# The joints of the first block: one wait for both norms' sums, three weights split ahead, two tiles grown together

## The chip, the cores and the metric

The kernel runs on one core of a Trainium2 chip. The metric is the device time of one execution in microseconds (us). Five engines work side by side, each through its own queue in order: PE (TensorE, matrix products), DVE (VectorE), ACT (ScalarE), POOL (GpSimd) and SP, which here only issues DMAs.

## The reference

Two stacks of layers run over 256 tokens of width 1024, in fp32. The first block has 16 extra "meta" tokens ahead (272 in all) and two layers, each a mixing layer and a feed-forward layer (FFN) with a convolution:

```python
for l in range(DEPTH):                       # DEPTH = 2
    u = _rms_norm(h, norm_mix_pre[l])
    (a_q, a_k, ..., gate_logits) = jnp.split(u @ w_in[l], offsets, axis=-1)
    ...                                      # four branches o_a, o_b, o_c, o_d
    merged = jnp.sum(jnp.einsum('btnw,nwd->btnd', branches, w_branch[l]) * gates, axis=2)
    h = h + _rms_norm(merged @ w_out[l], norm_mix_post[l])
    f = _conv_ffn(_rms_norm(h, norm_ffn_pre[l]), ffn_w_up[l], ffn_conv_w[l], ffn_conv_b[l], ffn_w_down[l])
    h = h + _rms_norm(f, norm_ffn_post[l])

def _rms_norm(x, g):
    y = x * lax.rsqrt(jnp.mean(x * x, axis=-1, keepdims=True) + NORM_EPS)
    return y * g
```

The second block (swiglu, convolution, pooling, and attention, under a condition vector) follows on the 256 tokens. What matters here is the pair of norms at every joint of the first block: norm 1 scales the result f of a layer's last product and adds it to h; norm 2 scales the new h for the first product of the next layer. There are four such joints: mixing to FFN and FFN to mixing in layer 0, mixing to FFN in layer 1, and FFN of layer 1 to the first swiglu of the second block.

## The kernel before, in words

Activations lie with the 1024 features on 128 partitions times 8 slices ("k") and the tokens along the free dimension. Every fp32 factor is split into a high and a low part: weights into wh and wl, inputs into uh and ul. A product is then three matmuls per slice: wh with uh, wh with ul, wl with uh. A 128x1024 weight tile (8 slices, 128 outputs) takes 24 matmuls.

Weights arrive by DMA as `raw` chunks of two tiles. ACT copies a tile into wh (`split`, L105), DVE takes the difference into wl (`split_low`, L118). `prefetch` (L129) does that ahead as long as a set of wh/wl is free: three sets (NS), plus "spare" ones in some stages. `get` (L154) hands over the next tiles. PSUM results are evicted by generators that `advance` (L178) moves on a step at a time. The written order of the code is the order of each engine's queue.

A joint goes as follows. `out_gemm` (L1524) makes the last product of a layer in 8 results j. `evict` writes f on ACT and, into a tile s, three sets of squares and products: f before the gain, squared; f squared; h times f. DVE adds those of j = 1 to 5 into the first. `post` then sums over the features with `summed` (L1577): matmuls with s as moving data and a column of ones as weights leave 32 equal rows, ACT copies them (L1590), and PE transposes them so that tokens lie on partitions (L1592). This is done first for norm 1, whose mean DVE scales (L269) and POOL raises to the power -1/2 (L271), then for the two sums of norm 2. `spread` (L274) turns the result r1 into a row for all partitions. For each slice k, DVE multiplies f (L1628), DVE or POOL adds it to h (L1630), ACT writes uh (`raw_hi`, L322) and DVE ul (`raw_lo`, L326).

`first_gemm` (L339) is the first product of the next layer. Its first group of tiles (`groups`: three tiles, or two in the second joint) runs on h times the gain, not yet scaled by norm 2 ("raw"), slice by slice as h comes. Meanwhile the power r2 is found. At the end of the group the inputs are written a second time, scaled (`normed`, L287, with `pr`, the spread r2), DVE scales the raw results (L385), and the remaining tiles run on the scaled inputs, one tile of 24 matmuls after another. `post` also ran `mid`, columns of the condition's modulation (`ada_some`, L1774, tiles adaw), which DVE makes in the out_gemm of the FFNs and in the swiglus.

## Time and profile before

| | us |
|---|---|
| median of 3 runs (2201.56 to 2204.61) | 2204.09 |
| profiled execution, own time | 2204.02 |
| its span, first to last instruction | 2202.0 |
| PE busy | 2137.4 (97%) |
| DVE busy | 1597.9 (73%) |
| mean granted clock of PE | 0.992 |

Times in the trace count from the start of the span. The four joints stand at 401 to 432, 615 to 653, 1005 to 1036 and 1207 to 1245 us. At full clock the matmuls of 272 columns begin 0.125 us apart, those of 256 columns 0.12 us; where the granted clock is 0.50, 0.226 us. A matmul's own 0.29 us overlap with those of its neighbours, so the pitch counts, not the sum of durations.

### The profile page before, as it was taken

How to read it: one execution, taken by the hardware profiler on the slowest of the kernel's cores; microseconds unless marked ns; L12 is line 12 of the kernel's file. 1: busy time of each engine (PE TensorE's matmuls, PEld its weight loads, DVE VectorE, ACT ScalarE, POOL GpSimd, SP SyncE). 2: the span in 40 equal slices, each digit the busy share in tenths (PEclk: the TensorE clock that was granted, in tenths of full speed). 3: DMA queues.
4: the chain of work that ended last, by engine and by line, in shares of the span. 5: the costliest groups of instructions: out<-in, count | busy, mean ns of one | idle time of the engine just before them, and what ended most of it. 6: DMA issues, size and time to landing. Idle time of an engine off the chain costs nothing. (4 is left out here: it accounts for less than half of the span.)

```text
span 2202.0 us, 42228 instructions
## 1 busy us (share of the span) xinstructions
PE 2137.4 (97%) x17234; PEld 2051.9 (93%) x17234; DVE 1597.9 (73%) x2833; ACT 1195.7 (54%) x2164; POOL 173.4 (8%) x223
## 2 busy tenths in 40 slices
PE   7999999999989999999999899999999999999998
PEld 7898989899979899898999899999999999989998
DVE  5665555888985656558989877797877877777553
ACT  4556454667456554547765644455544544476442
POOL 1320111100031101111000100001000000001000
PEclk9999999999999999999999999999999999999999
DMA  7653234454854342345559687555777687744552
GB/s 281 196 199 125 97 134 156 180 181 174 316 201 161 126 151 104 128 167 184 207 186 361 240 289 270 216 204 189 253 276 285 253 284 269 261 154 163 183 178 72
DMA packets 74322, 443.42 MB, mean 201 GB/s; under 512 B 14477, under 2 KB 15821, under 8 KB 26128
## 3 DMA queue, kind: packets, MB, share of 16 engines
q1 hardware_dynamic: 63312, 423.85, 53.7%
q0 software_dynamic: 10528, 16.79, 2.6%
q8 instruction: 135, 2.21, 0.4%
q14 instruction: 59, 0.48, 0.1%
q10 hardware_dynamic: 288, 0.07, 0.0%
HBM read 437.32 MB, written 10.01 MB: 203 GB/s over the span
## 5 line engine op out<-in xcount | busy, mean ns | idle before, releaser
L227 PE MATMUL g<-uh,wh 128*128 128x256 f32 (+2 forms) x3560 | 1028.0, 289 | 11.1 <-ACT uh L322 6.2
L227 PE MATMUL g<-ul,wh 128*128 128x256 f32 (+2 forms) x3560 | 1019.9, 286 | 10.8 <-DVE ul L326 6.3
L227 PE MATMUL g<-uh,wl 128*128 128x256 f32 (+2 forms) x3560 | 1016.6, 286 | 3.2 <-DVE wl L122 3.2
L122 DVE TENSOR_TENSOR wl<-raw,wh 128x1024 fp32r<-128x1024 f32 (+2 forms) x668 | 787.9, 1185 | 274.5 <-ACT wh L114 273.2
L114 ACT ACTIVATE wh<-raw 128x1024 fp32r<-128x1024 f32 (+2 forms) x668 | 678.3, 1020 | 348.3 <-PE g L227 313.7
L227 PEld LDWEIGHTS g<-uh,wh 128*128 128x128 f32 x3560 | 674.3, 189 | 34.1 <-issue 13.8
L227 PEld LDWEIGHTS g<-ul,wh 128*128 128x128 f32 x3560 | 673.1, 189 | 16.4 <-DVE ul L326 7.1
L227 PEld LDWEIGHTS g<-uh,wl 128*128 128x128 f32 x3560 | 675.1, 190 | 4.4 <-DVE wl L122 4.0
L227 PE MATMUL g<-gh,wh 128*128 128x256 f32 (+1 forms) x1056 | 299.2, 283 | 0.0
L227 PE MATMUL g<-gh,wl 128*128 128x256 f32 (+1 forms) x1056 | 299.2, 283 | 0.0
L227 PE MATMUL g<-gl,wh 128*128 128x256 f32 (+1 forms) x1056 | 299.0, 283 | 0.0
L227 PEld LDWEIGHTS g<-gl,wh 128*128 128x128 f32 x1056 | 201.5, 191 | 0.0
L227 PEld LDWEIGHTS g<-gh,wh 128*128 128x128 f32 x1056 | 201.3, 191 | 0.0
L227 PEld LDWEIGHTS g<-gh,wl 128*128 128x128 f32 x1056 | 201.3, 191 | 0.0
L1774 DVE CUSTOM_DVE_ANT_0 adaw<-adaw,condb,vec 128x1024 f32<-128x1024 f32 x144 | 182.4, 1279 | 0.0
L1677 DVE SCALAR_TENSOR_TENSOR y<-edge,vec,y 128x272 f32<-128x272 f32 (+1 forms) x176 | 86.4, 493 | 29.5 <-ACT y L1672 26.2
L227 PE MATMUL g<-oh,wh 128*128 128x272 f32 (+1 forms) x296 | 87.8, 297 | 0.0
L227 PE MATMUL g<-ol,wh 128*128 128x272 f32 (+1 forms) x296 | 84.8, 287 | 0.0
L227 PE MATMUL g<-oh,wl 128*128 128x272 f32 (+1 forms) x296 | 84.8, 286 | 0.0
L1920 ACT ACTIVATE sg<-g 128x256 f32<-128x256 f32 x80 | 30.5, 382 | 99.1 <-PE g L227 99.0
L1276 ACT ACTIVATE gt<-g 128x272 f32<-128x272 f32 (+1 forms) x64 | 25.1, 392 | 101.8 <-PE g L227 101.7
L1670 ACT ACTIVATE edge<-g 128x272 f32<-128x272 f32 (+1 forms) x82 | 32.3, 393 | 59.3 <-PE g L227 59.1
(384 smaller groups left out, 2311.5 us busy)
## 6 DMA issues: line engine op xcount, KB each, us to landing
raw<-in_weights_dram SPq DMA_DIRECT2D x298, 1024.0 KB, 5.0
adaw<-in_ada_t_dram SPq DMA_DIRECT2D x72, 1024.0 KB, 6.1
raw<-in_weights_dram SPq DMA_DIRECT2D x28, 768.0 KB, 5.0
skew<-scr POOLq DMA_DIRECT2D x6, 1086.0 KB, 23.0
h<-skew POOLq DMA_DIRECT2D x16, 272.0 KB, 3.7
h<-skew POOLq DMA_DIRECT2D x8, 512.0 KB, 5.2
condb<-cond SPq DMA_DIRECT2D x5, 512.0 KB, 4.7
hd<-h SPq DMA_DIRECT2D x2, 1088.0 KB, 8.9
```

Of the source, the lines that this page charges most:

```text
L114: self.nc.scalar.activation(h3[:, :, d0 : d0 + n], c.tile[:, :, c0 : c0 + n], AF.Copy)
L122: self.nc.vector.tensor_tensor(out=l3[:, :, d0 : d0 + n], in0=c.tile[:, :, c0 : c0 + n], in1=h3[:, :, d0 : d0 + n].bitcast(F32), op=SUB,)
L227: self.nc.tensor.matmul(out, lhsT, rhs, start=start, stop=stop, skip_group_check=True)
L1276: nc.scalar.activation(t[:, :rn], ps[:, :rn], AF.Tanh, scale=0.5)
L1670: nc.scalar.activation(e[:, 1 + r0 : 1 + r0 + rn], ps[:, :rn], AF.Copy)
L1677: nc.vector.scalar_tensor_tensor(out=y, in0=e[:, o : o + on], scalar=cw(i), in1=y, op0=MUL, op1=ADD)
L1774: self.nc.vector.tensor_tensor_reduce(out=t[:, i, :], in0=t[:, i, :], in1=self.condb, scale=1.0, scalar=self.v("ada_b_2", c), op0=MUL, op1 ...
L1920: nc.scalar.activation(t, ps[:, :SEQ], AF.Silu)
```

## The change

- **Sums.** DVE now adds the sets of all j (for norm 1 of j up to 5, the last two stay apart). Norm 1's sums are made with s as weights and the column of ones as moving data (`column`, 128x1), so they lie on partitions at once; the ACT copies and the transposes go. Norm 2's sums follow as six such columns, from the one accumulated tile, behind the spread.
- **Wait.** A copy `fence` on DVE stands behind the power. `warm` puts 2, 14 and 3 matmuls of 256 columns into a PSUM tile that nobody reads, between the sums and around the spread.
- **Weights.** The first three tiles of the next layer are split ahead into tiles of their own (`extra`, `places`): eh and el in the mixing stage, xwh/xwl and two of the adaw buffers in the FFN. The out_gemm's last piece splits up to four tiles; then `quiet` stops the prefetch until the raw group is over.
- **Raw group.** The slices from 4 on are scaled and added between the slices of the group (`steps`); per slice the group runs wh and wl with uh for its tiles, and wh with ul of the slice before. The power of norm 2 is asked for at k = 0, its spread stands at k = 5.
- **Groups.** The FFN's first gemm and the first swiglu's go from (3,) to (3, 2), the second mixing's from (2,) to (3, 2): after the raw group two tiles grow together, three matmuls of one and three of the other per slice.
- **Moved.** Pools are opened and closed, and the DMAs for it issued, after the raw group (`later`, `settle`). The modulation columns: 12 in place of 24 in each FFN, and 40, 32, 40, 8 in place of 32, 32, 32, 0 and the rest in the swiglus; 144 in all as before.

```diff
+            extra = self.extra.get(self.n_split)
+            spare = extra is None and c.spare > 0 and c.spare == self.phase and sum(out) < self.n_spare
+            if extra is None and not spare and len(out) - sum(out) >= NS:
                 break
             while c.tile is None and self.lows:
                 self.split_low()
             if c.tile is None:
                 break
-            self.split(self.n_split, spare)
-            self.where[self.n_split] = spare
+            self.split(self.n_split, spare, extra)
+            if extra is None:
+                self.where[self.n_split] = spare
...
-        self.prefetch(max(2, first + n - self.n_split + 1))
+        need = first + n - self.n_split
+        if need > 0 or not self.quiet:
+            self.prefetch(max(need, 0 if self.quiet else 2, 0 if self.quiet else need + 1))
...
+    def warm(self, ps, n):
+
+        if self.n_used in self.split_tiles:
+            w = self.split_tiles[self.n_used][0]
+            for _ in range(n):
+                self.mm(ps[: w.shape[2], :SEQ], w[:, 0, :], self.ul[:, KD - 1, META:T])
...
+            late = raw and g == 0 and len(self.steps) > 0
+            after = after or late
+            pss = [(self.gps if i < (2 if after else 3) else self.aps)() for i in range(size)]
...
+            def low(k):
+                for (w, m0, m1), ps in zip(tiles, pss):
+                    self.mm(ps[: m1 - m0, : n + c0], w[0][:, k, m0:m1], self.ul[:, k, t], False, k == KD - 1)
+
             for k in range(KD):
+                t = slice(c.start - c0, c.stop)
                 for (w, m0, m1), ps in zip(tiles, pss):
-                    self.mm3(
-                        ps[: m1 - m0, : n + c0], w, k, m0, m1, (self.uh, self.ul), k, c.start - c0, n + c0,
-                        k == 0, k == KD - 1,
-                    )
-                if raw and g == 0 and k == 1:
+                    o, xh, xl = ps[: m1 - m0, : n + c0], self.uh[:, k, t], self.ul[:, k, t]
+                    self.mm(o, w[0][:, k, m0:m1], xh, k == 0, False)
+                    if late:
+                        self.mm(o, w[1][:, k, m0:m1], xh, False, False)
+                        continue
+                    self.mm(o, w[0][:, k, m0:m1], xl, False, False)
+                    self.mm(o, w[1][:, k, m0:m1], xh, False, k == KD - 1)
+                if late:
+                    if k:
+                        low(k - 1)
+                    if self.steps:
+                        self.steps.popleft()()
+                    if k == 0:
+                        r, bl = sums()
+                    if k == KD - 1:
+                        low(k)
+                        self.settle()
+                        self.quiet = False
+                elif raw and g == 0 and k == 1:
                     r, bl = sums()
-                elif raw and g == 0 and k == 2:
+                if raw and g == 0 and k == (5 if late else 2):
...
+            raw_now, raw = raw, raw and g < len(groups) - 1 and not late
+            if not raw_now:
...
-            self.prefetch(2)
+            if late:
+                c0 = 0
+            self.prefetch(1 if late else 2)
...
-            cols(3552, 768, evs, groups=(2,) if first == "D" else ())
+            cols(3552, 768, evs, groups=(3, 2) if first == "D" else ())
...
+            if j == 0:
+                S["acc"] = s
+            elif j >= KD - 2:
+                S["late"] = S.get("late", []) + [s]
+            if j == KD - 1:
+                yield
...
+            if j:
+                acc, q = S["acc"], 0 if j < KD - 2 else 1
+                nc.vector.tensor_tensor(out=acc[:, q:3, c], in0=acc[:, q:3, c], in1=s[:, q:3, c], op=ADD)
...
+        def places(i):
+
+            if kt == KD:
+                return [self.q4(nm, F32R).rearrange("p a b -> p (a b)")[:, :1024] for nm in ("eh", "el")]
+            if i == 0:
+                return [self.ff.tile([128, 1024], F32R, tag=nm, name=nm, bufs=1) for nm in ("xwh", "xwl")]
+            t = self.ff.tile([128, 2, D], F32R, tag="adaw", name="ew", bufs=2)
+            return t[:, 0, :], t[:, 1, :]
...
+                    self.extra = {self.n_used + 2 * n_pieces + i: lambda i=i: places(i) for i in range(3)}
...
+                    if n == n_pieces - 1:
+                        self.prefetch(4 - 4 * i)
+                        self.quiet = True
                     (wt,) = self.get()
...
-            r1 = self.pow_rsqrt(summed([0], self.w1(), pt)[:, 0], nb, D, "r1")[:, :nb]
-            self.prefetch(1, ahead=3)
-            self.drain()
-            pt = self.aps()
-            sums = summed([1, 2], self.w1(), pt)
...
+            pw, ps = self.gps(), self.aps()
+            self.mm(ps[:, 0:4], self.ident, self.zero4, True, False)
+            for i, s in enumerate([S["acc"]] + S["late"]):
+                for b, (t0, n) in enumerate(bl):
+                    column(ps[:, b : b + 1], s[:, 0, :], t0, n, False, i == 2)
+                self.warm(pw, (0, 2, 14)[i])
+
+            g = self.pipes.popleft()
+            next(g)
+            next(g)
+            r1 = self.pow_rsqrt(ps[:, :nb], nb, D, "r1")[:, :nb]
+            fence = self.sm.tile([128, 4], F32, tag="fence", name="fence", bufs=2)
+            nc.vector.tensor_copy(fence[:, :nb], r1)
+            for _ in g:
+                pass
             p1 = self.spread(r1, bl)
+            ps2 = self.aps()
+            for q in range(2):
+                for b, (t0, n) in enumerate(bl):
+                    column(ps2[:, 4 * q + b : 4 * q + b + 1], S["acc"][:, 1 + q, :], t0, n, True, True)
+            self.warm(pw, 3)
...
+            def step(k):
+                def fn():
+                    if k < KD:
+                        value(k, nc.gpsimd)
+                    self.raw_lo(k - 2)
+
+                return fn
+
+            self.before_norm(gain(), shift and shift(), c, second, [step(k) for k in range(4, KD + 2)])
             if shift:
                 self.raw_shift(self.mod[:, 0:8])
-            for k in range(KD):
-                nc.vector.tensor_tensor(out=f[:, k, c], in0=f[:, k, c], in1=p1[:, c], op=MUL)
-                eng = nc.gpsimd if k else nc.vector
-                eng.tensor_tensor(out=self.h[:, k, c], in0=self.h[:, k, c], in1=f[:, k, c], op=ADD)
-                self.raw_hi(k)
-                if k == 2:
-                    R["r2"] = second()
-                if k > 1:
-                    self.raw_lo(k - 2)
-            self.raw_lo(KD - 2)
-            self.raw_lo(KD - 1)
+            value(0, nc.vector)
+            value(1, nc.gpsimd)
+            self.raw_lo(0)
+            value(2, nc.gpsimd)
+            value(3, nc.gpsimd)
+            self.raw_lo(1)
...
-                self.add(self.gemm(x, one * 3, ev, r0, rn, groups=(3,)), *[ch for _, ch in begun], cg)
+                self.add(self.gemm(x, one * 3, ev, r0, rn, groups=(3, 2)), *[ch for _, ch in begun], cg)
...
-            lambda: self.ada_some(2),
+            lambda n: self.ada_some(2 if n < 2 else 1 if n < 10 else 0),
...
-            c = {(0, 0): 48, (0, 2): 80, (1, 0): 112}.get((i, s))
-            self.ada_begin(range(c, c + 32) if c else ())
+            self.ada_begin(range(*{(0, 0): (24, 64), (0, 2): (64, 96), (1, 0): (96, 136), (1, 2): (136, 144)}[i, s]))
...
+                self.add(self.gemm(x, m * 3, ev3, META, SEQ, groups=(3, 2)), *[ch for _, ch in begun], cg)
```

PE, from the last product of mixing 0 (g, the last wl) to the first raw matmul, before (a are PSUM tiles, s4 the squares, ones32 the ones, r1 the power):

```order
L227 MATMUL g_4587<-uh_81,wl_4551 128x272
L1584 MATMUL a_4660<-s4_4405,ones32_90 32x272
L1584 MATMUL a_4660<-s4_4619,ones32_90 32x272
L1584 MATMUL a_4660<-s4_4655,ones32_90 32x272
L1592 MATMUL a_4658<-ident_89,w1_4659 128x32 x3
L1584 MATMUL a_4680<-s4_4405,ones32_90 32x272 x2
L1584 MATMUL a_4680<-s4_4619,ones32_90 32x272 x2
L1584 MATMUL a_4680<-s4_4655,ones32_90 32x272 x2
L1592 MATMUL a_4678<-ident_89,w1_4679 128x64 x3
L227 MATMUL a_4691<-ident_89,r1_4670 128x16
L227 MATMUL a_4691<-ident_89,r1_4670 128x128 x2
L227 MATMUL g_4760<-uh_81,wh_4588 128x272
L227 MATMUL g_4760<-ul_82,wh_4588 128x272
```

After (eh, el are the tiles split ahead; the rows into g_4670 are the `warm` ones):

```order
L245 MATMUL g_4593<-uh_81,wl_4553 128x272
L245 MATMUL a_4671<-zero4_94,ident_89 128x4
L245 MATMUL a_4671<-ones32_90,s4_4407 128x1 x3
L245 MATMUL a_4671<-ones32_90,s4_4637 128x1 x3
L245 MATMUL g_4670<-ul_82,eh_4555 128x256 x2
L245 MATMUL a_4671<-ones32_90,s4_4667 128x1 x3
L245 MATMUL g_4670<-ul_82,eh_4555 128x256 x14
L245 MATMUL a_4708<-ident_89,r1_4703 128x16
L245 MATMUL a_4708<-ident_89,r1_4703 128x128 x2
L245 MATMUL a_4712<-ones32_90,s4_4407 128x1 x6
L245 MATMUL g_4670<-ul_82,eh_4555 128x256 x3
L245 MATMUL g_4736<-uh_81,eh_4555 128x272
L245 MATMUL g_4736<-uh_81,el_4556 128x272
```

Three 32-row sums, three transposes, six more sums and three more transposes stood ahead of the spread; now nine columns and sixteen `warm` matmuls do, and six columns behind it.

PE, the end of the raw group and what follows in the FFN of layer 0, before:

```order
L227 MATMUL g_4762<-uh_81,wh_4672 128x272
L227 MATMUL g_4762<-ul_82,wh_4672 128x272
L227 MATMUL g_4762<-uh_81,wl_4673 128x272
L227 MATMUL g_4904<-uh_81,wh_4757 128x272
L227 MATMUL g_4904<-ul_82,wh_4757 128x272
L227 MATMUL g_4904<-uh_81,wl_4758 128x272
L227 MATMUL g_4904<-uh_81,wh_4757 128x272
L227 MATMUL g_4904<-ul_82,wh_4757 128x272
L227 MATMUL g_4904<-uh_81,wl_4758 128x272
```

After:

```order
L245 MATMUL g_4737<-ul_82,eh_4594 128x272
L245 MATMUL a_4738<-ul_82,eh_4597 128x272
L245 MATMUL g_4922<-uh_81,wh_4600 128x272
L245 MATMUL g_4922<-ul_82,wh_4600 128x272
L245 MATMUL g_4922<-uh_81,wl_4601 128x272
L245 MATMUL g_4923<-uh_81,wh_4903 128x272
L245 MATMUL g_4923<-ul_82,wh_4903 128x272
L245 MATMUL g_4923<-uh_81,wl_4904 128x272
L245 MATMUL g_4922<-uh_81,wh_4600 128x272
L245 MATMUL g_4922<-ul_82,wh_4600 128x272
```

Before, 24 matmuls of the fourth tile follow each other; now the fourth tile's first three are followed by three of the fifth (wh_4903, wl_4904).

ACT at the same place, after (the last of the eight scaled inputs, the fifth tile's wh, the results' evictions, the sixth's wh):

```order
L322 ACTIVATE uh_81<-w1_4884 128x272
L322 ACTIVATE uh_81<-w1_4888 128x272
L322 ACTIVATE uh_81<-w1_4892 128x272
L127 ACTIVATE wh_4903<-raw_4586 128x1024
L1754 ACTIVATE edge0_4856<-w1_4897 128x272
L1756 ACTIVATE y_4908<-w1_4897,vec_100 128x272
L1754 ACTIVATE edge1_4857<-w1_4899 128x272
L1756 ACTIVATE y_4911<-w1_4899,vec_100 128x272
L1754 ACTIVATE edge2_4858<-w1_4901 128x272
L1756 ACTIVATE y_4914<-w1_4901,vec_100 128x272
L127 ACTIVATE wh_4916<-raw_4586 128x1024
```

Before, at that place on ACT:

```order
L304 ACTIVATE uh_81<-w1_4863 128x272
L304 ACTIVATE uh_81<-w1_4867 128x272
L304 ACTIVATE uh_81<-w1_4871 128x272
L114 ACTIVATE wh_4882<-raw_4581 128x1024
L114 ACTIVATE wh_4885<-raw_4581 128x1024
L1670 ACTIVATE edge0_4748<-w1_4876 128x272
L1672 ACTIVATE y_4893<-w1_4876,vec_98 128x272
```

The fifth tile's wh stands behind the eight scaled inputs in both orders; before, it was the first of two.

## Rows read from the trace of the kernel before

**Rows 1.** The page's busy times over the whole span.
```profile
PE 2137.4 (97%) x17234; PEld 2051.9 (93%) x17234; DVE 1597.9 (73%) x2833; ACT 1195.7 (54%) x2164; POOL 173.4 (8%) x223
```

**Rows 2.** PE's waits: line waited at, releaser, us in total, times, longest.
```profile
PE g L227 <- DVE ul L326: 6.3, 4, 1.6
PE g L227 <- ACT uh L322: 6.2, 4, 1.6
PE a L1592 <- ACT w L1590: 3.9, 8, 0.5
PE g L227 <- DVE wl L122: 3.2, 3, 1.2
PE a L701 <- ACT dv L993: 1.6, 1, 1.6
```

**Rows 3.** The first transition's timeline: start, duration, engine, line, operation, [idle before].
```profile
401.19 0.29 PE L227 MATMUL g<-uh,wl 128*128 128x272 f32 x1
...
404.10 1.00 POOL L271 TENSOR_TENSOR r<-ms,mhalf 128x3 f32<-128x3 f32 x1 [26.94 <-DVE ms L269]
...
406.21 1.03 PE L227 MATMUL a<-ident,r 16*128 16x16 f32 x6
407.28 0.44 DVE L1628 TENSOR_TENSOR f<-f,a 128x272 f32<-128x272 f32 x1 [1.68 <-PE a L227]
...
408.80 0.40 PE L227 MATMUL g<-uh,wh 128*128 128x272 f32 x1 [1.56 <-ACT uh L322]
```

**Rows 4.** Windows, first and third transition: length, busy by engine, granted clock, DMA.
```profile
410.64:414.05 3.41, 3.27 (x14) 3.27 (x15) 3.41 (x9) 1.06 (x3) 3.41 (x5) 0.50 0.00 0
414.06:422.20 8.14, 8.14 (x65) 7.97 (x64) 7.07 (x21) 4.67 (x10) 1.83 (x2) 1.00 0.65 205
...
427.50:431.90 4.40, 4.40 (x23) 4.40 (x24) 4.29 (x8) 4.38 (x10) 0.00 (x0) 0.61 0.47 147
...
1029.40:1033.50 4.10, 2.96 (x24) 2.75 (x24) 4.03 (x7) 4.10 (x9) 0.00 (x0) 1.00 0.44 138
```

**Rows 5.** Timeline, first transition, from the last normed input to the fifth tile.
```profile
424.36 0.43 ACT L304 ACTIVATE uh<-w 128x272 fp32r<-128x272 f32 x1 [0.33 <-DVE w L302]
...
424.70 1.99 ACT L114 ACTIVATE wh<-raw 128x1024 fp32r<-128x1024 f32 x2
...
425.18 1.13 DVE L385 TENSOR_TENSOR w<-g,pr 128x272 f32<-128x272 f32 x3
...
426.23 2.35 DVE L122 TENSOR_TENSOR wl<-raw,wh 128x1024 fp32r<-128x1024 f32 x2
...
427.50 0.43 PE L227 MATMUL g<-uh,wl 128*128 128x272 f32 x1 [1.19 <-DVE wl L122]
```

**Rows 6.** Timeline, second transition: a modulation column, first raw matmul, two waits.
```profile
617.86 1.28 DVE L1774 CUSTOM_DVE_ANT_0 adaw<-adaw,condb,vec 128x1024 f32<-128x1024 f32 x1
...
623.67 0.39 PE L227 MATMUL g<-uh,wh 128*128 128x272 f32 x1 [1.56 <-ACT uh L322]
...
640.39 0.39 PE L227 MATMUL g<-uh,wl 128*128 128x272 f32 x1 [0.84 <-DVE wl L122]
...
652.98 0.44 PE L701 MATMUL a<-ident,dv 128*128 128x128 f32 x2 [1.59 <-ACT dv L993]
```

**Rows 7.** Timeline and windows, fourth transition.
```profile
1211.51 0.14 DVE L269 TENSOR_SCALAR ms<-a 128x2 f32<-128x2 f32 x1
...
1223.86 4.63 DVE L122 TENSOR_TENSOR wl<-raw,wh 128x1024 fp32r<-128x1024 f32 x4 [0.46 <-ACT wh L114]
...
1216.19:1223.00 6.81, 5.44 (x25) 5.44 (x26) 6.16 (x16) 3.67 (x8) 5.85 (x8) 0.50 0.40 168
1229.00:1236.00 7.00, 5.36 (x26) 3.39 (x24) 6.50 (x18) 3.94 (x8) 0.00 (x0) 1.00 0.39 162
1239.00:1245.00 6.00, 5.80 (x50) 5.60 (x48) 4.86 (x7) 5.41 (x9) 0.00 (x0) 1.00 0.60 195
```

**Rows 8.** The same windows' columns, most of the next stage.
```profile
1250.00:1500.00 250.00, 247.73 (x2070) 246.21 (x2068) 208.27 (x337) 125.20 (x189) 3.82 (x3) 1.00 0.68 242
```

More of the change, by code (lines that the diff above doesn't have):

```diff
@@ L79, in add, with later, settle @@
         self.items.append((fn, chunks))
+    def later(self, fn):
+        self.items.append((lambda: self.deferred.append(fn), ()))
+    def settle(self):
+        while self.deferred:
+            self.deferred.pop(0)()
     def start_stream(self):
@@ L103, in pump_dma, with split @@
             self.n_dma += 1
-    def split(self, j, spare):
+    def split(self, j, spare, extra=None):
         c, s = self.subq[j]
@@ L138, in prefetch @@
             out = [x for k, x in self.where.items() if self.held or k >= self.n_used]
-            spare = c.spare > 0 and c.spare == self.phase and sum(out) < self.n_spare
-            if not spare and len(out) - sum(out) >= NS:
+            extra = self.extra.get(self.n_split)
+            spare = extra is None and c.spare > 0 and c.spare == self.phase and sum(out) < self.n_spare
+            if extra is None and not spare and len(out) - sum(out) >= NS:
                 break
@@ L367, in first_gemm @@
                     nc.scalar.activation(pr, ps[:, o : o + n], AF.Copy)
-                elif k in (4, 6):
+                elif not late and k in (4, 6):
                     self.prefetch(1)
@@ L371, in first_gemm @@
                 yield
-            self.held = False
-            if not raw:
+            self.held, self.norm = False, None
+            raw_now, raw = raw, raw and g < len(groups) - 1 and not late
+            if not raw_now:
                 for i, ps in enumerate(pss):
@@ L379, in first_gemm @@
                 continue
-            if g == len(groups) - 1:
+            if not raw:
                 self.normed(self.h[:, :, c], pr, gain, shift, n, (self.uh[:, :, c], self.ul[:, :, c]))
@@ L411, in setup @@
         nc.vector.memset(self.zero, 0.0)
+        self.zero4 = c.tile([128, 4], F32, name="zero4")
+        nc.vector.memset(self.zero4, 0.0)
         self.mhalf = c.tile([128, 16], F32, name="mhalf")
@@ L756, in pool_open @@
             S["merged"] = self.mx.tile([128, KD, T], F32, tag="merged", name="merged", bufs=1)
-        self.add(pool_open)
+        (self.later if l else self.add)(pool_open)
         if l == 0:
@@ L779, in pre @@
             nc.sync.dma_start(out=self.hd[l], in_=self.h)
-        self.add(pre)
+        (self.later if l else self.add)(pre)
         def to(name, i, w=128):
@@ L1512, in mixing @@
         )
-        self.add(lambda: self.mx_guard.__exit__(None, None, None))
+        self.later(lambda: self.mx_guard.__exit__(None, None, None))
     def down_chunks(self, w, kt):
@@ L1661, in pool_open @@
                 nc.vector.memset(t[:, T + 1 : T + 2], 0.0)
-        self.add(pool_open)
+        self.later(pool_open)
         def conv(j, ps):
@@ L1718, in conv_ffn @@
         self.add(self.ada_end)
-        self.add(lambda: self.ff_guard.__exit__(None, None, None))
+        self.later(lambda: self.ff_guard.__exit__(None, None, None))
     def out_gemm_ff(self, w, S, o0, on, l):
@@ L1877, in gated_gemm @@
             return
-        for ch, j0, k0, nk, first, last in self.down_chunks(w, kt):
+        for n, (ch, j0, k0, nk, first, last) in enumerate(self.down_chunks(w, kt)):
             def fn(j0=j0, k0=k0, nk=nk, first=first, last=last):
@@ L1898, in gated_gemm @@
             self.add(fn, ch)
-            if kt == KF:
-                self.ada_some()
+            if kt == KF and n < 10:
+                self.ada_some(2)
     def swiglu(self, i, s, f, nxt):
@@ L1934, in swiglu, with ev3 @@
             cu = self.wcols(self.w["ffn_w_up_2"][i, f], j * 128, 256)
+            if j == 0 and i + s == 0:
+                begun = [(evg, cg), (evu, cu)]
+                continue
+            if j == 2 and i + s == 0:
+                def ev3(q, ps, evs=[e for e, _ in begun] + [evg]):
+                    return evs[q // 2](q % 2, ps)
+                self.add(self.gemm(x, m * 3, ev3, META, SEQ, groups=(3, 2)), *[ch for _, ch in begun], cg)
+                self.add(self.gemm(x, m, evu, META, SEQ), cu)
+                self.ada_some(2)
+                continue
             if j == 0:
@@ L1937, in both @@
                     return (evg if q < 2 else evu)(q % 2, ps)
-                self.add(self.gemm(x, m + m, both, META, SEQ, groups=(4,) if i + s else (3,)), cg, cu)
+                self.add(self.gemm(x, m + m, both, META, SEQ, groups=(4,)), cg, cu)
                 continue
@@ L2359, in opened @@
             self.xp, self.n_spare, self.phase = self.xp_guard.__enter__(), 5, phase
-        self.add(opened)
+        self.later(opened)
         for i in range(2):
```

74 lines of the change are left out of this document (33 added, 41 removed).

## The prediction

> **What bounds the kernel now.** The page's busy times come first: PE works 97% of the span [rows 1]. Nearly all the time is matmuls that the change leaves alone, so only stretches where PE waits or runs at half clock can give anything. The list of PE's waits says where these are [rows 2]: at the four joints PE waits 1.6 us each for the first uh and 1.6 us each for the first ul, the ACT copies ahead of the transposes add 3.9 us over eight waits, and the weights' low parts 3.2 us over three. That is 19.6 us over all joints, under 1% of the time; beside it stands the half clock. Then the timelines of the joints show which engine each wait hangs on [rows 3, 5, 6, 7], and the windows what PE does there and at what clock [rows 4, 7].
>
> In the first joint the last product starts at 401.19, the power at 404.10, the spread at 406.21 and the first raw matmul at 408.80 [rows 3]. Then PE stands until 410.78 for ul and runs at half clock (0.50, which is 1.2 of 2.4 GHz) for 3.4 us, 14 matmuls [rows 4]. The raw group's 72 matmuls are issued by 422.2. The scaled inputs are written meanwhile, the last uh at 424.36; only behind it does ACT split the fifth tile and the sixth, and DVE their low parts, so PE waits until 427.50 with 98 of 120 matmuls done (72 raw, 24 of tile four, 2 of tile five) [rows 5]. The rest runs at a mean clock of 0.61 [rows 4] and the 120th matmul is through at 431.9. I use the 120th matmul as the mark for each joint, since after it PE goes on without waits in the FFNs.
>
> **The change part by part.** The sum is made against the profiled execution's own time, 2204.02 us (span 2202.0), which stands 0.07 us below the median of 2204.09; nothing has to be moved between the two.
>
> *Sums and wait, joints one and three.* The ACT copies, the transposes and the 32-row sums go. What comes instead: a zeroing and nine columns. No row shows a column behind these squares; between the pitch of a matmul (0.12) and the 0.26 of a 32-row sum (six in 1.56) the ten cost 1.2 to 2.6 us; I take 2.2. They can't start at once: DVE has splits in its queue and only then the adds of the accumulated squares, by about 402.2 (a low part costs 1.2 us [rows 5], and one more of them stands there than before). So columns end near 404.5, mean 0.16, power 1.00 [rows 3], that is 405.7. But the 14 warm matmuls stand on PE ahead of the spread: 404.5 + 14 x 0.12 = 406.2, the same as before. The first raw matmul comes at 408.8 again, between 0.5 us earlier and 0.5 later. The fence costs DVE nothing by itself, since DVE has only the spread to wait for; at most the two last adds, 0.9 us, are late, and they feed norm 2, which is needed much later.
>
> *Raw group.* Six matmuls per slice need uh alone, so the wait for ul goes, and with PE fed the clock should stay full. The bound is then POOL's chain of h, 0.9 us per slice with a power of 1.0 between, and the late spread at slice 5. By this chain the raw group ends at 420.4 in place of 422.2.
>
> *Two tiles together.* Here the order of the queues decides [the rows of order above]. After the raw group PE has three matmuls of the fourth tile and then meets the fifth, whose wh stands on ACT behind the eight scaled inputs as before. These are paced by DVE and start when `pr` is there, 418.4 against 418.6. So wh is ready about 425.6 (424.7 + 1.0 of the two in 1.99), wl behind the three scaled results about 427.3 (426.23 + half of 2.35, less 0.1) [rows 5]. Before, PE used the time from 422.2 to 425.8 for the whole fourth tile; now it stands. At 427.3 it has done 72 + 3 + 2 = 77 of 120, and 43 remain: 43 x 0.125 = 5.4 us at full clock, 432.7, which is 0.8 us later than before. If the clock falls as in 427.50 to 431.90 (0.61 over 4.4 us [rows 4]), 4.4 x 0.39 = 1.7 us more. Joint one: +0.8 to +2.5, and I take +2.
>
> *Joint three* is the same with one difference: before, it kept full clock over its wait of 1.2 us (3.2 less 1.19 and 0.84 [rows 2, 5, 6]) and after it (1.00 over 1029.40 to 1033.50 [rows 4]) and was through at 1033.5. With wl at 1030.8 the change is through at 1030.8 + 5.4 = 1036.2, or 1.7 later. +2.7 to +4.4; I take +3.2.
>
> *Joint two.* The mean waited behind two modulation columns of 1.28 us [rows 6]; these go, and the spread is then bound by the warm matmuls, 1 us earlier than before. Five tiles are ready here (three ahead and two in ordinary sets, since the FFN's own spare set holds one of the last product's), so the two tiles together don't stand: first raw matmul 622.6 (623.67 [rows 6] less 1), raw group 11.6 us as in joint one (408.8 to 420.4), to 634.3, 48 more matmuls to 640.3, the 120th. Before, it came at 646.2 after a split's wait until 640.39 [rows 6]. Of these 5.9 us most is given back: the sixth and seventh tiles are split behind the scaled inputs, and the chain ACT-DVE-ACT of the keys to dv, which ended at 652.98 [rows 6], moves only as far as its own work lets it, to about 650. That is 3 us, less 1.7 if PE's rest brings the half clock. -1.3 to -3; I take -2.2.
>
> *Joint four.* Two columns go from before the mean (1211.51), so f starts 2.3 us earlier; the stretch of 6.8 us at clock 0.50 [rows 7], 25 matmuls, would run at full; and four low parts in a row, 4.63 us, no longer delay the scaled inputs. The raw group, some 10.6 us with 258 columns, ends at 1224.0 in place of 1229, the two ready tiles to 1229.8. Then PE waits for the sixth tile, whose low part follows the three scaled results: about 1233.1. 48 x 0.12 = 5.8 gives 1238.9, or 1240.4 with some half clock, for the 168th, which before came at 1244.6 and a wait of 0.4 later (last window of [rows 7]). -4.6 to -6.2; I take -5.
>
> *Moved work.* 24 modulation columns move from the FFNs to the second block, 24 x 1.28 = 31 us of DVE. There PE is busy 247.7 of 250 us and DVE 208.3 [rows 8]; 8 more columns in that stage are 10 us, which leaves DVE at 88%. Cost nothing; without the cover up to 1.28 us for each late tile. DMAs that move behind the raw group (condition, modulation, the edge of h) pass only each other on SP and POOL; the weight chunks, three ahead, are freed earlier. The group of tiles in the swiglu and its tables cost the same matmuls.
>
> Sum: +2 + 3.2 - 2.2 - 5 = -2.0, so 2202.0. The ends: +0.8 + 2.7 - 3 - 6.2 = -5.7 and, with another 0.5 us at each first matmul, +2.5 + 4.4 - 1.3 - 4.6 + 1 = +2.0: 2198.3 to 2206.0.
>
> **The rivals.** *A: the joints keep what they gain.* The gain at the 120th matmul stays in joints two and four (-5.9; 1239 to 1229.8 = -9.2), and one and three lose only 0.8 and 2.7: -11.6, 2192.4. For it speaks that PE is the bound after every joint [rows 1, 8]; against it the chain to dv in joint two and the sixth tile's split, which stand behind the same scaled inputs. 17%.
>
> *B: slower, by the clock.* The longer rests, some 6 us in joints one and three and 3 us in two and four, could each be followed by as long a stretch at 0.50 as joint four has, 6.8 us [rows 7], and not by 3.4. That costs 3.4 us per joint: +4.2, +6.1, +0.4, -2.8, together +7.9, 2211.9. It decides once PE stays at half clock for a second stretch of that length. For it: the longest rests of PE in any joint stand here. Against it: joint three's wait of 1.2 us brought no half clock at all [rows 4]. 15%.
>
> The Trainium skill ("TensorE: Matmul & The Clock Gate", Part 1) says that a PE left idle falls to 1.2 GHz and, kept busy, comes back to 2.4 GHz; by that rule each of the new rests ends at half clock, as rival B has it, and the warm matmuls help only ahead of the raw group. The trace agrees in joints one, two and four and not at joint three's second wait.
>
> *C: the change doesn't do what it says.* POOL's h paces the raw group whatever PE does, now with a second power early in its queue; PE rests in each slice and the raw group ends as before. Then joint one and three stay at +2 and +3.2 (they hang on the fifth tile, not on the raw group), joint two gives -1 and joint four -3: +1.2, 2205.2. For it: POOL is busy all of 410.64 to 414.05 (3.41 of 3.41 [rows 4]). Against it: that stretch's PE is at half clock and short of ul too. 16%.
>
> **How the numbers follow.** 52% for the forecast, 17, 15 and 16 for A, B and C. A measurement of this kernel can tell 0.2%, 4.4 us, from no change; that is 2199.6 and 2208.5. Faster: all of A and a quarter of the forecast's cases (those with joint four near -6 and joint one near +1), 0.17 + 0.13 = 0.30. Slower: two thirds of B and a little of C, 0.10 + 0.03 = 0.13. The rest, 0.57, is the same. For 8 in 10 the range covers the forecast's own 2198.3 to 2206.0 and C, half of A and most of B: 2194 to 2210.
>
> **What would show it.** Right: in the FFNs' first gemm PE stands about 6 us after three matmuls of the fourth tile, waiting for ACT's wh and DVE's wl; the waits for ul after the first raw matmul are gone; the clock is 1.00 in the raw groups; the first swiglu's 168th matmul comes about 5 us earlier against the last product before it. Wrong: if the fifth tile is ready when the raw group ends (then joints one and three gain, too), if the second block shows PE waiting for modulation or splits, or if the half clock follows the rests for 6.8 us.

## The result, and the profile after

The changed kernel takes 2225.11 us (median of 4 runs, 2221.83 to 2225.97) against 2204.35 us before: a ratio of 1.0096, 95% interval 1.0081 to 1.0111. It is slower by some 21 us, outside the range forecast. The profiled execution of after is the quickest of the four, 2221.83 us with a span of 2219.8; against the 2202.0 of before that is 17.8 us.

By the page's busy times PE has 8.7 us more [rows 1], about what the 76 warm matmuls ask for at 0.12 us each (9.1, an estimate); so 9 of the 17.8 us are PE standing still.

```profile
PE 2146.1 (97%) x17334; PEld 2071.8 (93%) x17334; DVE 1603.7 (72%) x2851; ACT 1194.3 (54%) x2156; POOL 173.9 (8%) x223
```

PE's waits, as in [rows 2] (line waited at, releaser, us in total, times, longest):

```profile
PE g L245 <- ACT wh L127: 11.2, 3, 4.7
PE a L245 <- ACT s L1600: 8.8, 2, 4.5
...
PE a L757 <- ACT dv L1049: 3.9, 1, 3.9
PE g L245 <- DVE wl L135: 3.8, 5, 0.9
...
PE g L245 <- DVE sg L2008: 2.4, 1, 2.4
PE g L245 <- ACT uh L348: 2.3, 10, 0.4
```

What the change was to remove is removed: the raw groups' waits for ul and those for the ACT copies no longer stand there, and that for uh falls from 6.2 to 2.3 us. But 11.2 us for a weight's wh are new, and 8.8 us for s, the squares of the last results, and 2.4 us for sg, which DVE makes from the first swiglu's results; only then are their PSUM tiles free. The largest two are worth a look at their places.

Joint two, ACT's timeline (start, duration, operation, [idle before]):

```profile
617.70 1.06 ACT L127 ACTIVATE xwh<-raw 128x1024 fp32r<-128x1024 f32 x1 [9.65 <-PE g L245]
618.66 1.99 ACT L127 ACTIVATE ew<-raw 128x1024 fp32r<-128x1024 f32 x2
620.56 1.99 ACT L127 ACTIVATE wh<-raw 128x1024 fp32r<-128x1024 f32 x2
622.45 0.38 ACT L1600 ACTIVATE s<-g 128x272 f32<-128x272 f32 x1
```

And PE's, at the same place:

```profile
622.88 1.44 PE L245 MATMUL a<-ones,s 128*128 128x1 f32 x6 [4.30 <-ACT s L1600]
...
625.89 3.33 PE L245 MATMUL g<-ul,xwh 128*128 128x256 f32 x14
629.15 1.39 PE L245 MATMUL a<-ident,r 16*128 16x16 f32 x6
```

Before, ACT had its splits done and wrote the last squares 0.3 us after the last product (615.70):

```profile
616.02 0.40 ACT L1542 ACTIVATE s<-g 128x272 f32<-128x272 f32 x1 [0.22 <-PE g L227]
```

In the changed kernel ACT stands 9.65 us before it may write xwh, until the last product (617.50) is through: xwh is the FFN's spare set, and the last tile of the out_gemm lies in it. Behind this one instruction stand four more splits, 5 us in all, and behind these the squares of the last results, which the columns want. Then the fourteen warm matmuls run at half clock, 3.33 us in place of 1.9, and the spread behind them starts 2 us after the power is done (626.30 + 0.86). Joint four shows the same (xwh from 1220.55, a wait of 4.5 us).

Joint one goes the way the prediction told, within 0.2 us, until the fifth tile is there: 26.2 us after the last product, forecast 26.1. PE's wait behind the raw group, and the clock around it, in views that answer to [rows 5] and [rows 4]:

```profile
424.45 0.59 PE L245 MATMUL g<-uh,wh 128*128 128x272 f32 x1 [4.69 <-ACT wh L127]
...
426.15 0.60 PE L245 MATMUL g<-uh,wl 128*128 128x272 f32 x1 [0.88 <-DVE wl L135]
```

```profile
407.75:419.20 11.45, 10.87 (x80) 10.03 (x79) 10.21 (x30) 4.95 (x11) 6.68 (x8) 1.00 0.22 49
419.20:426.15 6.95, 1.38 (x7) 0.83 (x5) 6.72 (x17) 5.26 (x12) 0.00 (x0) 0.69 0.72 297
426.15:434.30 8.15, 8.15 (x44) 8.15 (x45) 5.31 (x9) 4.67 (x7) 0.00 (x0) 0.64 0.37 131
1015.73:1019.14 3.41, 3.41 (x16) 3.21 (x16) 0.94 (x3) 0.00 (x0) 0.86 (x1) 0.50 0.33 135
```

The raw group runs at full clock, as forecast. Then PE does 7 matmuls in 6.95 us, and the 44 that follow take 8.15 us at a mean clock of 0.64; before, a mean of 0.61 lasted for 4.40 us [rows 4]. In joint three the clock falls already ahead of the raw group (fourth line), is back for it, and falls again in the wait for the fifth tile.

To compare versions I count, in each joint, from the start of the last product's last matmul to the moment when the next gemm's first 264 matmuls (raw group included) are done, read as the start of the 265th. "At the 120th" and "at the 168th" are read in the same way. By then each kernel has done the same work. These times are read from each version's trace:

| us to the 264th matmul | joint 1 | joint 2 | joint 3 | joint 4 | sum |
|---|---|---|---|---|---|
| before | 48.9 | 55.1 | 45.5 | 49.4 | 198.8 |
| after | 52.4 | 62.1 | 51.4 | 53.7 | 219.6 |
| e1 own buffer | 52.6 | 54.1 | 54.6 | 47.0 | 208.3 |
| e2 one by one | 51.2 | 62.0 | 50.3 | 49.6 | 213.0 |
| e3 fifth first | 47.2 | 63.6 | 50.8 | 56.4 | 218.1 |
| e4 = e1 + e3 | 47.2 | 56.4 | 50.8 | 49.9 | 204.3 |
| e5 = e4, no warm | 47.8 | 56.7 | 47.9 | 50.4 | 202.8 |
| e6 = e4, swiglu as before | 48.7 | 56.7 | 49.2 | 44.6 | 199.2 |
| e7 before, in twos | 52.5 | 55.1 | 49.8 | 50.1 | 207.4 |
| e8 = e6, no warm | 47.8 | 57.2 | 47.6 | 44.3 | 196.9 |
| e9 = e8, raw group of 2 | 47.8 | 53.4 | 47.7 | 44.6 | 193.3 |
| e10 before, columns moved | 47.3 | 55.0 | 45.5 | 47.8 | 195.5 |
| e11 joint 4 alone | 47.2 | 54.6 | 47.1 | 44.2 | 193.0 |

The sum after is 20.8 us over that of before; 3 us come back between the joints, where the trace of before has two stretches of 3.4 us at half clock (from 820.24 and 1970.54) that the trace of after has not. One joint's time in one trace is good to 1.5 us at best: joint one has the same instruction order in before and e10 and reads 48.9 and 47.3, and joint three has it in after and e1 and reads 51.4 and 54.6, with half clock at other places.

Each version was timed beside the kernel before, whose median was 2204.35 us beside the changed kernel, 2201.39 beside e1 to e4, 2202.54 beside e5 to e8 and 2202.01 beside e9 to e12. Versions of different groups are therefore compared by what each has over its own before; the changed kernel has 20.8 us.

### The profile page after: what moved, and what is told of

Read it like the earlier page. It is cut to its first block, busy times and chain, and to the rows that moved or that the text cites. A ratio compares the mean times of both kernels' runs of the same rounds, so it can differ in the third digit from the quotient of the medians.

```text
span 2219.8 us, 42473 instructions
## 1 busy us (share of the span) xinstructions
PE 2146.1 (97%) x17334; PEld 2071.8 (93%) x17334; DVE 1603.7 (72%) x2851; ACT 1194.3 (54%) x2156; POOL 173.9 (8%) x223
## 5 line engine op out<-in xcount | busy, mean ns | idle before, releaser
L245 PE MATMUL g<-uh,wh 128*128 128x256 f32 (+2 forms) x3464 | 1000.8, 289 | 18.0 <-ACT wh L127 11.2
L245 PE MATMUL g<-ul,wh 128*128 128x256 f32 (+2 forms) x3464 | 988.9, 285 | 2.8 <-DVE ul L1560 2.8
L245 PE MATMUL g<-uh,wl 128*128 128x256 f32 (+2 forms) x3464 | 985.8, 285 | 3.8 <-DVE wl L135 3.8
L135 DVE TENSOR_TENSOR wl<-raw,wh 128x1024 fp32r<-128x1024 f32 (+4 forms) x656 | 772.1, 1182 | 261.9 <-ACT wh L127 261.2
L127 ACT ACTIVATE wh<-raw 128x1024 fp32r<-128x1024 f32 (+4 forms) x656 | 665.6, 1019 | 343.6 <-PE g L245 298.4
L245 PEld LDWEIGHTS g<-uh,wh 128*128 128x128 f32 x3464 | 653.6, 189 | 39.9 <-issue 16.0
L245 PEld LDWEIGHTS g<-uh,wl 128*128 128x128 f32 x3464 | 656.0, 189 | 5.4 <-DVE wl L135 5.0
L245 PEld LDWEIGHTS g<-ul,wh 128*128 128x128 f32 x3464 | 654.5, 189 | 4.1 <-DVE ul L1560 3.7
L2003 ACT ACTIVATE sg<-g 128x256 f32<-128x256 f32 x80 | 30.6, 382 | 100.0 <-PE g L245 100.0
```

The costliest lines, as they stand in the source:

```text
L127: self.nc.scalar.activation(h3[:, :, d0 : d0 + n], c.tile[:, :, c0 : c0 + n], AF.Copy)
L135: self.nc.vector.tensor_tensor(out=l3[:, :, d0 : d0 + n], in0=c.tile[:, :, c0 : c0 + n], in1=h3[:, :, d0 : d0 + n].bitcast(F32), op=SUB,)
L245: self.nc.tensor.matmul(out, lhsT, rhs, start=start, stop=stop, skip_group_check=True)
L2003: nc.scalar.activation(t, ps[:, :SEQ], AF.Silu)
```

## The experiments

**e1.** Joints two and four: another buffer for the first weight split ahead (and `y` 6, `gg` 4 buffers, for room).

```diff
-                return [... for nm in ("xwh", "xwl")]
+                return [... for nm in ("zwh", "zwl")]
```

> One edit at joints two and four: the first of the three weights split ahead gets a buffer of its own in place of the spare set's, which the last product's last tile still holds (y from 8 to 6 buffers and gg from 6 to 4 make room for it). Theory 1: in the changed kernel ACT waits for the end of the last product before it may write that first weight (617.70 in joint two), and four more splits and then the last results' squares stand behind it; with a buffer of its own the splits run before the product ends, and the first column after the wait comes about 5 us earlier in joints two and four: spread about 6 us after the last product in place of 11.65 and 10.55, total about -9 us, near 2216. Rival 1: it is the five splits as such (5.1 us of ACT) that hold the squares, whenever they may start, because the raw chunks come late: then under 2 us change, 2223 or more. Rival 2: what costs is the half clock after PE's rests; then the spread comes earlier but the 264th matmul does not, and the time moves by less than 3 us.

Measured: 2211.60 us (6 runs), 1.0045 [1.0031, 1.0060] of before. That is 10.2 us over its before, 10.6 less than the changed kernel has. The spread comes 4.33 us after the last product in joint two (11.65) and 4.63 in joint four (10.55). ACT's timeline of this run shows why:

```profile
608.23 1.04 ACT L127 ACTIVATE zwh<-raw 128x1024 fp32r<-128x1024 f32 x1
...
614.77 1.06 ACT L127 ACTIVATE wh<-raw 128x1024 fp32r<-128x1024 f32 x1 [1.74 <-DMA raw<-in_weights_dram]
615.84 0.40 ACT L1600 ACTIVATE s<-g 128x272 f32<-128x272 f32 x1
```

The five splits are the same five, in the same place of the queue, and done before the product's last matmul at 617.78. So it was the buffer and not the five splits as such: theory 1 holds, both rivals fall. The two joints give 14.6 us; joint three, where this run's order is that of after, is 3 us worse, with 13.65 us at half clock from 1007.70 on.

**e2.** `groups=(3, 2)` back to `(3,)` in the FFNs' first gemm.

> One edit at joints one and three: the first gemm of the FFN goes back to one tile after another behind the raw group (groups (3,)); the rest of the change stays. Theory 1: what joints one and three lose is the interleave with a fifth tile that is split only behind the scaled inputs; without it PE does the fourth tile's 24 matmuls during the wait, the 120th matmul comes about 4 us earlier after the last product (30 in place of 34.3 in joint one, 30 in place of 34.2 in joint three), total about -8 us, near 2217. Rival: the half clock takes it back (10 us of half clock in joint one stays, since PE still rests), then -2 us or less in all. Rival: a fourth tile alone is paced by the scaled inputs and the sixth tile comes no earlier, then the 168th matmul stands where it stood and nothing is gained.

Measured: 2214.23 us, 1.0056 [1.0041, 1.0071], 12.8 us over its before, 8 less than after, but not where it was expected: joints one and three give 1.2 and 1.1 us, joint four 4. In joint one the stretch from the 72nd to the 168th matmul is 4.3 us shorter (16.8 against 21.1), as theory 1 has it, and the stretch up to the end of the raw group 3 us longer, with half clock for 10.24 us from 403.78. And the edit did more than meant: with another count of tiles the sets turn otherwise, and xwh is free at 608.30 after a wait of 2.15 us, so that the spread comes at 5.17 and 3.57 in joints two and four. It is a second witness for what the buffer does to the spread, but joint two keeps nothing of it (62.0 in place of 62.1): PE then waits 4.7 us for another wh and 2.8 for dv. For the groups it is a poor witness; e7 asks for these alone.

**e3.** The next tile split ahead of the scaled inputs.

```diff
+            if late:
+                self.prefetch(1)
+                while self.lows:
+                    self.split_low()
             if not raw:
                 self.normed(
```

> One edit in the first gemm: the next tile (the fifth in joints one and three, the sixth in two and four) is split ahead of the scaled inputs in place of behind them; tiles still grow in twos. Theory 1: PE's wait of about 6 us goes from joints one and three; the scaled inputs start about 1 us later (one low part of 1.2 us on DVE ahead of them), both tiles follow them, the 120th matmul comes 8 us earlier in each (about 26 in place of 34), of which 4 us are given back to the sixth tile's low part, which still stands behind six evictions: 168th about 36 in place of 40; total -8 to -10 us, near 2216. In joint two the sixth tile comes a little earlier, -1 us. Rival: the clock; if half clock follows any joint, the total moves by less than 4 us.

Measured: 2223.22 us, 1.0097 [1.0082, 1.0112]: 21.8 us over its before, no gain on after, a miss. Joint one does what was expected (120th matmul 26.95 us after the last product in place of 34.33, 168th 35.2), and PE's waits for wh are gone. Joint three gives 7 us between the 72nd and the 120th matmul, of which 5 are left at the 168th, and loses 4.4 ahead of the 72nd, with half clock for 13.65 us from 1012.74. Joints two and four lose 1.5 and 2.8 us; that the scaled inputs are only pushed back there is likely, but no run takes it apart.

**e4.** Both edits.

> The own buffer of joints two and four and the tile split ahead of the scaled inputs together. Theory 1: the gains are of different joints and add up, -17 to -19 us, near 2207, about the time of the kernel before. Rival (clock): less than the sum of the two.

Measured: 2208.19 us (9 runs), 1.0028 [1.0017, 1.0039]: 6.8 us over its before, 14 less than after, and short of the 17 expected. The separate edits gave 10.6 and -1, so together they give more than their sum; the intervals are too wide to say how much. Against e1 joints one and three gain 5.4 and 3.8 us, and joints two and four lose 2.3 and 2.9, as in e3. What is left against before lies mostly in joint three (+5.3).

**e5.** e4 without the warm matmuls (`self.warm(pw, 0)`).

> The version with both repairs (own buffer, tile split ahead of the scaled inputs) without the 76 warm matmuls. Theory 2: where the clock falls before the raw group (joint three of that version: half clock from 1004.87 on), the fourteen warm matmuls take 3.3 us in place of 1.9 and stand ahead of a spread whose power was done 2 us before, and the three others stand ahead of the first raw matmul; at full clock they still end 0.6 us behind the power. Without them the spread follows the power: 2 us earlier in joint three, 0.6 in the others, total -3 to -5 us, near 2204. Rival: the warm matmuls keep the clock; without them the raw groups run at half clock in all joints, each 72nd matmul comes 1.5 to 4 us later, total 2212 or more.

Measured: 2208.00 us (10 runs), 1.0023 [1.0014, 1.0033]: no difference to e4 in the time. Both sides of the expectation are seen and cancel: joint three's spread comes 4.74 us after the last product in place of 7.71, its 264th matmul 2.9 us earlier; but half clock now begins within 1.6 us of the spread in all four joints (6.8, 6.8, 10.2 and 6.8 us), where in e4 the raw groups of joints one, two and four had none, and these three joints lose 0.3 to 0.6 us each. So the warm matmuls do keep the clock there; it is worth little.

**e6.** e4 with the first swiglu's groups as before.

> The version with both repairs, with the first swiglu's first gemm as in the kernel before: a raw group of three of four tiles, the fourth alone, none grown in twos. Theory 1: joint four gains 7 us at the 120th matmul and gives all of it back at the 168th, since the two results of the second group wait behind six low parts on DVE and the PSUM tiles come free late (PE waits 5.4 us for sg); with the old grouping the splits come one by one, and the 264th matmul comes about 3.5 us earlier (46 after the last product in place of 49.9): near 2204.5. Rival: sg waits because the weight chunks come late, whatever the grouping: no change, 2207 to 2209.

Measured: 2202.95 us (10 runs), 1.0003 [0.9993, 1.0012]: 5 us under e4, and joint four's 264th matmul comes 5.3 us earlier. PE's longest wait between 1206 and 1262, first of e4:

```profile
PE g L245 <- DVE sg L2012: 5.4, 1, 5.4
```

then of e6:

```profile
PE g L245 <- ACT uh L324: 1.2, 1, 1.2
```

The wait for sg goes with the grouping; the rival (late chunks) falls.

**e7.** The kernel before with the fourth and fifth tile of the FFN grown together.

```diff
-            if g == len(groups) - 1:
+            if g == 0:
                 self.normed(
...
             first += size
+            raw = False
...
-                self.add(self.gemm(x, one * 3, ev, r0, rn, groups=(3,)) ...
+                self.add(self.gemm(x, one * 3, ev, r0, rn, groups=(3, 2)) ...
```

> The kernel before with one part of the change alone: in the FFNs' first gemm the fourth and fifth tile grow together behind the raw group of three. Theory 1: PE stands where the fifth tile's wh and wl are not there, as in the changed kernel; the 120th matmul comes 1 to 4 us later in joints one and three (30.7 and 28.3 before), total +3 to +8 us, 2204 to 2209. Rival: in the kernel before the wait is covered, since its raw group ends later (21 in place of 19.3 us after the last product): +1 us or less.

Measured: 2210.26 us, 1.0037 [1.0023, 1.0051]: +7.7 us, +3.6 in joint one and +4.3 in joint three. Of PE's waits between 405 and 440 two are for the fifth tile:

```profile
PE g L227 <- ACT wh L114: 2.1, 1, 2.1
...
PE g L227 <- DVE wl L122: 1.2, 1, 1.2
```

This part alone makes the kernel before as slow in joint one as the whole change does (52.5 and 52.4), and shows the prediction's mechanism without the rest of the change around it. How the loss divides between the wait itself and the half clock around it (6.83 us from 427.02 and from 1031.18) isn't taken apart.

**e8.** e6 without the warm matmuls.

> Both of the two edits on the version with both repairs: no warm matmuls, and the first swiglu's groups as before. If the two gains are of different joints they add up: -6 to -8 us against that version, near 2201, which cannot be told from the kernel before. Rival (the clock): without warm matmuls joint four runs its raw group at half clock and the sum is less.

Measured: 2202.21 us (10 runs), 0.9999 [0.9989, 1.0008]. As with e5, no warm matmul is missed in the time. The parts found so far to cost something are now taken out, and the rest is worth nothing over all.

**e9.** e8 with `groups=(2,)` in the second mixing's first gemm, as before.

> The version e8 (both repairs, no warm matmuls, old swiglu groups) with the second joint's first gemm as in the kernel before: a raw group of two tiles, the others alone. Theory: joint two gains 2 to 4 us at the 120th matmul and gives it back where PE waits 4 us for dv, whose chain on ACT and DVE starts with three results at once behind the raw group of three; with two at once it starts as in the kernel before, 264th matmul near 54.5 after the last product in place of 57.2: -2.5 us, near 2200. Rival: the raw group of two is paced by the sums of h, as long as one of three, and the third tile's work comes on top: +1 to +3 us.

Measured: 2198.43 us (10 runs), 0.9981 [0.9972, 0.9990]: 3.6 us under its before (e8: 0.3), joint two's 264th matmul at 53.4 in place of 57.2. The wait of 4 us for dv is gone from the list; the rival falls.

**e10.** The kernel before with the modulation columns as in the change: `range(12 * l, 12 * l + 12)` and two, one or no column per piece in the FFN; 40, 32, 40, 8 in the swiglus.

> The kernel before with one part of the change alone: the modulation columns moved (12 in place of 24 in each FFN, none in the last pieces; 40, 32, 40, 8 in the swiglus). Theory 1: this is what joints two and four gain at their first matmul: DVE is free for the mean, joint two's spread 1 us and joint four's 2.3 us earlier after the last product, the 168th matmul in joint four about 36 in place of 37.9; nothing is lost in the second block: -2 to -4 us, near 2200. Rival: the columns cost DVE in the second block what they save, no change.

Measured: 2199.26 us (11 runs), 0.9986 [0.9977, 0.9995]: 2.75 us faster than before. Joint four's spread comes at 4.65 in place of 6.25 us and its 168th matmul at 36.3 in place of 37.9; joint two's spread 0.4 us earlier. Joints two and four account for 1.7 us of it in the table; another 1.5 stand in joint one, whose order is the same and whose half clock lies elsewhere. Of the two parts that were tried alone (this one and e7's) it is the one that gains.

**e11.** The stage change in joint four alone, the rest as before, columns moved.

```diff
+        if kt == KD or l == 0:
+            return self.out_gemm_old(w, kt, x, r0, rn, new_f, gname, l, gain, shift, mid)
```

> The stage change in joint four alone (as in e8: own buffer, next tile split ahead of the scaled inputs, no warm matmuls, old swiglu groups) and the moved modulation columns; joints one to three as in the kernel before. Theory: joints one and three gain nothing from the change even when repaired, joint three loses 2 to 4 us to the half clock that comes with its columns and waits, joint four gains 5; so this is the best of the versions: -5 to -6 us, near 2197. Rival: the old joints were as fast only by luck of the clock; then no better than e8, 2200 to 2203.

Measured: 2195.19 us (6 runs), 0.9972 [0.9961, 0.9984]: 6.8 us faster than before, where the changed kernel is 20.8 slower. Against e10, which has the columns alone, it is 4.1 us, and joint four 3.6 (44.2 against 47.8). It has the lowest median of all versions; its interval overlaps that of e9.

**e12.** e8 without the `fence` copy.

> The version e8 without the copy that holds DVE beside the power of norm 1. The question is only the power itself: 0.86 us with the fence in the changed kernel, 1.00 before. If DVE's work beside it is what slows it, 1.00 again in joints one to three; if not, 0.86. The time does not tell (0.14 us by four joints).

Measured: 2205.0 us (one run, which tells nothing of the time). Norm 1's power in joint one, first of e8, then of e12:

```profile
404.49 0.86 POOL L289 TENSOR_TENSOR r<-ms,mhalf 128x3 f32<-128x3 f32 x1 [27.40 <-DVE ms L287]
```

```profile
403.74 1.28 POOL L289 TENSOR_TENSOR r<-ms,mhalf 128x3 f32<-128x3 f32 x1 [27.40 <-DVE ms L287]
```

It is 1.28, 1.28, 1.25 and 1.10 us in the four joints without the fence and 0.86, 0.86, 0.86 and 0.71 with it. The fence shortens it, by more than expected. But it isn't DVE's work as such: the power of norm 2, with DVE busy beside it all the time, takes 0.86 us in the first three joints of both runs. What stands beside norm 1's power in e12 is one instruction, the add of the sums (`s<-s,s`, 403.58 to 404.30), begun before it, and the power ends 0.72 us after that add does.

## Why the prediction was wrong

*Joint two and joint four: forecast -2.2 and -5, measured +7.0 and +4.3 at the 264th matmul (joint four +2.7 at the forecast's own mark, the 168th).* The step that failed is "f starts 2.3 us earlier" in joint four and "1 us earlier" in joint two. It took the modulation columns away from DVE, rightly (e10), and set nothing in their place. But the weights split ahead are instructions more in ACT's queue ahead of the last results, and the first of them goes into "the FFN's own spare set", of which the prediction itself said, in the paragraph on joint two, that it "holds one of the last product's". It read from this that more ordinary sets are free, and not that the write must wait for that product. So ACT stood 9.65 us, and the spreads came 11.65 and 10.55 us after the last product, against 5.38 and 6.25 before. e1 settles it: another buffer, the splits in the same order, and the spreads come 7.3 and 5.9 us earlier.

*Joint four's second half: "the two ready tiles to 1229.8", then -5 at the 168th.* With the buffer mended (e1) joint four gains 2.4 us at both the 168th and the 264th matmul. The sixth tile's wait, which the prediction did have, is followed by one for sg that it had not; without it (e6) the gain is 4.8. That this is the size forecast is luck: e6 has none of the two tiles grown together that the forecast's sum counts on.

*Joint two: "most is given back".* This part was right in kind: with the buffer mended 6.1 us are gained at the 120th matmul (24.5 against 30.6) and 1.0 kept at the 264th, less than the 1.3 at the forecast's end, because of dv. e9 shows that the wait for dv comes with the raw group of three.

*Joints one and three: forecast +2 and +3.2, measured +3.5 and +5.9.* In joint one the mechanism was right in every step (first matmul 0.2 us later, raw group done 1.8 us earlier, then a stand of 5.6 us at the fifth tile) and e7 shows its last step alone. Mis-sized was the clock's term: "1.7 us more" in joint one, where half clock lasts 10.2 us, from 421.81 on, in place of the 3.4 that the row of before suggested; the 43 matmuls that are left take 8.1 us and not 5.4 at full clock, 2.7 more. In joint three "the same with one difference" failed at the first step: half clock comes ahead of the raw group as well, at 1015.73, and the warm matmuls, which take nearly twice as long then (3.34 us against 1.92), stand in PE's queue ahead of the spread. It comes 7.0 in place of 4.9 us after the last product, and the fifth tile 1.9 us later than forecast; half clock behind it (6.83 us from 1036.21) costs 1.4 more.

*Rivals.* A falls with the late spreads. C falls too: joint one's raw group is done 19.25 us after the last product, as forecast (19.2), and not at 21.0 as before. B (slower, by the clock) named the side. Its condition came true, since each joint has a stretch at half clock of 6.8 us or more, but it forecast 7.9 us and not 20.8. Over the joints PE has 47.8 us at half clock in place of 20.5; in e1 it is still 44.4, and yet the joints are 11.3 us shorter. With e7's 7.7 us for the tiles grown together, most of the loss has a cause that a run shows apart; part of e7's share is the half clock around its wait. Of the Trainium skill ("TensorE: Matmul & The Clock Gate", Part 1) the trace after agrees that an idle PE falls to 1.2 GHz: each of the four joints has a rest that ends at a clock of 0.50. The warm matmuls keep the clock in part: with them (e4) the joints have 27.3 us at half clock, half of it in joint three, without them (e5) 44.4, and the time is the same. What stays open is why the same order has its half clock in other places and lengths from run to run: joint one has none in e3 and e4 and 3.4 us in e6, joint three 10.2 in after and 20.5 in e1.

## What to carry to other kernels

An instruction moved ahead is moved ahead of everything behind it in its queue; before pricing it, ask which buffer it writes, who reads that buffer last, and what stands behind it. Tiles that grow together need all their inputs at the first step, tiles that grow one by one only their own; the former pays only where all are split. A gain at the first matmul of a stage is not the stage's gain until the next late thing has passed: mark a place behind it, compare there, and undo the parts one by one, since one part of a slow change can be worth keeping (here the moved columns and joint four, together -6.8 us).

## What was not expected of the hardware

POOL's power on 128x3 numbers took 0.86 us with DVE idle beside it, and 1.25 to 1.28 us where an add of DVE had begun just before it (e8, e12); beside the DVE work that goes with norm 2's power in these two runs it took 0.86 us again. And in joint three of the changed kernel, e1, e3, e4 and e6, a PE stand of 1 us ahead of one-column matmuls (six columns take 1.5 us) was followed by half clock ahead of the raw group; the 32-row sums of before, at the same place, were not, and the clock fell at 1014.80, inside the raw group. That the columns are the reason is not shown: joint one has the same columns behind a stand of 0.67 us, and its clock fell ahead of the raw group in e1, e2 and e6 and not in after, e3 and e4.
